# Strassen's algorithm for half the columns of an MLP's second projection, with the scale of u applied earlier

## The chip, the cores and the metric

The kernel runs on one core of one Trainium2 chip. A core has TensorE (PE in the profile, with its weight loads as PEld), VectorE (DVE), ScalarE (ACT), GpSimd (POOL), and SyncE (SP), whose queue issues nearly all the DMAs here. The metric is the device time of one execution in microseconds; lower is better.

## The reference

Two layers of an encoder on x of 256 tokens by 2048. Each layer adds to x the output projection of three kinds of attention heads, then a squared-ReLU MLP; a final RMSNorm ends it. What the change touches is the MLP:

```python
x = x + jnp.einsum('bse,ed->bsd', mix, w_o[l])
h = rmsnorm(x, norm_mlp[l])
u = jax.nn.relu(jnp.einsum('bsd,df->bsf', h, w_up[l]))
x = x + jnp.einsum('bsf,fd->bsd', u * u, w_down[l])
```

w_up is 2048 x 8192 and w_down 8192 x 2048 per layer, all in float32.

## The kernel before

**Precision.** Every float32 operand is split into a high part (a cast to fp32r) and a low part (the rest). A product of two is three matmuls: high by high, low by high, high by low. Weights are split on the chip: `split` (L829 to L839) casts 128x1024 values on ScalarE (L836, `whi`) and subtracts on VectorE (L837, `wlo`).

**Steps.** The whole kernel is a list of steps, one for each 512 KB of weights: 128 partitions by 1024 values. The main loop (from L868) goes through them in order. For step i it loads raw weights (`wraw`, six buffers) up to step i + 6, splits up to step i + 1 into pairs of `whi` and `wlo` (four pairs), and then issues the step's matmuls. Between the steps, `tick` issues pieces of other work from a queue. The framework orders each engine's instructions by its own priorities from this order of issue, so the orders printed below are those of the built programs.

**The MLP.** There are 256 tokens, two blocks t of 128. The 8192 inner columns go in eight groups g of 1024. An *up step* takes two row blocks of 128 and 512 inner columns of w_up, which gives u transposed, in four banks: eight matmuls of 512 columns (high and low of h side by side) and eight of 256 (L644, L648). After eight up steps the result is added up, squared with relu (L659), and split into u's high and low parts in `uT`, one tile for 256 inner columns, so four tiles for a group (q in the new code counts them through the layer). A *down step* takes 256 inner rows (one tile of `uT`, index k) by 512 output columns (index j) of w_down. With the three products, two row blocks and two token blocks it is twelve matmuls of 512 columns, all through `mode_b` (the matmul is L465). After four steps, the two banks are added to x on VectorE (L684), scaled by r2, one over the mean square of x: since relu is squared, the norm's scale can come after.

The order is the up steps of group 0, then for each g the 16 up steps of group g + 1 and the 16 down steps of group g. One may also read it as 16 down steps of a group followed by the 16 up steps of the group after the next. The normed h comes in eight tiles `hT2`, two for each of the four 512-column pieces of x (`hprep`, TensorE transposes at L210, ScalarE L218, VectorE L221).

**PSUM.** Six single banks (tag `bank`) serve as `mm` and `tr` tiles, and two more as one tile `S` for attention scores, or in the MLP for half of the up steps.

Of the kernel before, what the change touches and what calls it, by code (L numbers as in the profile page):

```python
# [23 lines left out]
P = 128  # L24
D = 2048
# [18 lines left out]
def tile_trunk(ctx: ExitStack, tc: tile.TileContext, x_in, w_in, w_o, w_up, w_down,  # L44
               gains, rowp, t5, rpb, gfin, cst, onehot, out):
    nc = tc.nc
    LOOK_LOAD, LOOK_SPLIT, BUDGET = 7, 2, 2.2
    N_WARM = 6
    D_X, D_S, D_SS, D_T, D_PV, D_QK, D_RQ, D_RK, D_SQ = 6.0, 6.0, 7.0, 18.0, 6.0, 6.0, 24.0, 16.0, 6.0
# [17 lines left out]
    def mid(dt, *shape):  # L67
        return dp.tile([P, *shape], dt, tag="mid", bufs=6, name=nm("mid"))

# [22 lines left out]
    ones = cp.tile([P, 64], F32, name="ones")  # L92
    nc.vector.memset(ones, 1.0)
# [349 lines left out]
    def mix_rs(l, grp, acc, done):  # L443
        ps = tr_bank()
        for t in range(NT):
            nc.tensor.matmul(ps[:, t * 64:(t + 1) * 64], acc[:, t * P:(t + 1) * P], ones, start=True, stop=True)
# [9 lines left out]
    class Step:  # L456
        def __init__(self, src, kk, n, pre, mm):
            self.src, self.kk, self.n, self.pre, self.mm = src, kk, n, pre, mm

    def mode_b(banks, h_tile, wh, wl, sub, first, last, n=512, blocks=(0, 1)):  # L460

        def one(t, i, part):
            kk = sub[i]
            a = h_tile[i][:, int(part == "lh"), kk, t * P:(t + 1) * P]
            return nc.tensor.matmul(banks[t][:, 0:n], a, (wl if part == "hl" else wh)[:, i, :],  # L465
                                    start=first and i == 0 and part == "hh",
                                    stop=last and i == len(sub) - 1 and part == stop).ins
        if hook[0]:
            stop = "hl"
            for part in ("hh", "lh", "hl"):  # L470
                with pinned():
                    ins = [one(t, i, part) for t in blocks for i in range(len(sub))]
                last_pe[0] = ins[-1]
                if part == "hh":
                    hook[0]()
            return
        stop = "lh"
        for t in blocks:
            for i in range(len(sub)):
                for part in ("hh", "hl", "lh"):  # L480
                    one(t, i, part)
# [3 lines left out]
    def layer_steps(l):  # L485
# [6 lines left out]
        def mlp_rs():  # L492
            st["r2"] = small(2)
            nc.vector.reciprocal(st["r2"], mean_eps(st["ss2"], 4, 1.0 / D))
# [130 lines left out]
        uT = {}  # L625

        def up_steps(g):
            for c in range(2):
                fc = 2 * g + c
                box = {}  # L630
                for k in range(8):
                    def pre(k=k):
                        need((("mlp", l), k))

                    def mm(wh, wl, k=k, c=c, fc=fc, box=box):
                        if k == 0:
                            box["b"] = [mm_bank() for _ in range(2 if c else 4)]
                            if c:
                                sb = score_banks().rearrange("p (b i) n -> p b (i n)", i=2)
                                box["b"] += [sb[:, 0], sb[:, 1]]  # L640
                        ht = st["hT2"][k]
                        for kk in range(2):
                            for fs in range(4):
                                nc.tensor.matmul(box["b"][fs], wh[:, kk, fs * P:(fs + 1) * P], ht[:, kk, :],  # L644
                                                 start=k == 0 and kk == 0, stop=False, skip_group_check=True)
                        for kk in range(2):
                            for fs in range(4):
                                nc.tensor.matmul(box["b"][fs][:, 0:256], wl[:, kk, fs * P:(fs + 1) * P],  # L648
                                                 ht[:, kk, 0:256],
                                                 start=False, stop=k == 7 and kk == 1, skip_group_check=True)  # L650
                        if k == 7:
                            for b in range(2):

                                a = mid(F32, 512)
                                for i in range(2):
                                    o, ai = box["b"][2 * b + i], a[:, i * 256:(i + 1) * 256]
                                    nc.scalar.copy(ai, o[:, 256:512])
                                    nc.vector.tensor_add(ai, ai, o[:, 0:256])
                                nc.vector.scalar_tensor_tensor(a, a, 0.0, a, op0=ALU.max, op1=ALU.mult)  # L659
                                u = big(F32R, 2, 2, 256)  # L660
                                uf = u.rearrange("p s k c -> p s (k c)")
                                nc.scalar.copy(uf[:, 0, :], a)
                                nc.vector.tensor_sub(uf[:, 1, :], a, f(uf[:, 0, :]))  # L663
                                uT[2 * fc + b] = u
                    steps.append(Step(w_up[l, fc * 8 + k], 2, 512, pre, mm))

        def down_steps(g):
            for j in range(4):
                box = {}
                for k in range(4):  # L670
                    def mm(wh, wl, j=j, k=k, box=box):
# [5 lines left out]
                        mode_b(box["b"], hts, wh, wl, [0, 1], k == 0, k == 3, blocks=(0,) if final else (0, 1))  # L677
# [4 lines left out]
                        def evac(t):  # L682
                            xs = x[:, t, j * 512:(j + 1) * 512]
                            nc.vector.scalar_tensor_tensor(xs, box["b"][t], st["r2"][:, t:t + 1], xs,  # L684
                                                           op0=ALU.mult, op1=ALU.add)
                        if final:
# [3 lines left out]
                            for c in range(2):  # L690
                                cols = slice(c * 256, c * 256 + 256)
                                for i, (hts, vh, vl) in enumerate(box["w"]):
# [3 lines left out]
                                nc.vector.scalar_tensor_tensor(xs, tail[c][:, 0:256], st["r2"][:, 1:2], xs,  # L696
                                                               op0=ALU.mult, op1=ALU.add)
# [7 lines left out]
                    steps.append(Step(w_down[l, (g * 4 + j) * 4 + k], 2, 512, None, mm))  # L705

        up_steps(0)
        for g in range(8):
            if g < 7:
                up_steps(g + 1)  # L710
            down_steps(g)
# [47 lines left out]
    def bias_a(kv):  # L759
        tb = sp.tile([P, 4, 384], F32, tag="bias", bufs=2, name=nm("biasA"))  # L760
        nc.sync.dma_start(tb, bass.AP(tensor=avec.tensor, offset=avec.offset + kv * 4 * 512,
                                        ap=[[1, P], [512, 4], [1, 384]]))
        return tb

    def g_unit(l, st, kind, kv, qb, qT, kh, kl, V, bias=None, rq=None):
# [5 lines left out]
        u.bias = lambda b: bias[:, 2 * b:2 * b + 2, qb * P:qb * P + 256][:, :, ::-1]  # L771
# [12 lines left out]
    def b_unit(l, st, h0, qT, kh, kl):  # L784
# [6 lines left out]
        tb = sp.tile([P, 2, 6 * 127], F32, tag="bias", bufs=2, name=nm("biasB"))  # L791
        for rr in range(2):
            off = ((l * 8 + h0) * 15 + rr + 4) * 127
            nc.sync.dma_start(tb[64 * rr:64 * rr + 64, :, 0:699], bass.AP(
                tensor=rpb.tensor, offset=rpb.offset + off, ap=[[1, 64], [15 * 127, 2], [1, 699]]))
        tc_ = big(F32, 2, 6, 64)
        for h in range(2):
            nc.gpsimd.tensor_add(tc_[:, h], tb[:, h].rearrange("p (a b) -> p a b", b=127)[:, :, 0:64],
                                 mask_b.rearrange("p (o d) -> p o d", o=1).to_broadcast([P, 6, 64]))
# [20 lines left out]
    raw_t, hi_t, lo_t = {}, {}, {}  # L820

    def load(i, halves=False):
        s = steps[i]
        w = wp.tile([P, s.kk, s.n], F32, tag="wraw", bufs=6, name=nm("wraw"))
# [5 lines left out]
    def split(i):  # L830
        s = steps[i]
        w = raw_t.pop(i)
        h = wp.tile([P, s.kk, s.n], F32R, tag="whi", bufs=4, name=nm("whi"))
        lo = wp.tile([P, s.kk, s.n], F32R, tag="wlo", bufs=4, name=nm("wlo"))
# [7 lines left out]
    nl = ns = 0  # L842
# [8 lines left out]
    for i in range(1, 8):  # L851
        load_x(i * 256, (i + 1) * 256)
        if i < 6:
            load(i)
    nl = 6
# [8 lines left out]
    for i, s in enumerate(steps):  # L864
# [17 lines left out]
        while ns < min(len(steps), i + LOOK_SPLIT):  # L882
            split(ns)
            ns += 1
        s.mm(hi_t.pop(i), lo_t.pop(i))
        hook[0] = None
        if i == 2:
# [61 lines left out]

def _pack_inputs(inp):  # L950
# [11 lines left out]
    o["w_up"] = np.stack([np.concatenate([_pack(a["w_up"][l][:, j * 512:(j + 1) * 512], 2) for j in range(16)])  # L962
                          for l in range(L)])
    o["w_down"] = np.stack([np.concatenate([
        _pack(a["w_down"][l][g * 1024:(g + 1) * 1024, j * 512:(j + 1) * 512], 2)
        for g in range(8) for j in range(4)]) for l in range(L)])
# [41 lines left out]
```

## Time and profile before

| | us |
|---|---|
| three runs, median (lowest to highest) | 2056.87 (2056.75 to 2056.89) |
| the profiled execution, its own time | 2057.3 |
| the profiled execution, its span | 2055.5 |
| ScalarE busy (share of the span) | 1049.3 (51%) |
| GpSimd busy (share of the span) | 255.7 (12%) |
| HBM bytes read | 377.34 MB |

The span is from the first to the last instruction; the execution's own time is 1.8 us longer. The page's busy rows give for each engine its time at work. Matmuls are pipelined, and their ends are modelled, so a single 128x512 matmul is shown as 0.39 us long though the next starts 0.23 us after it: how fast TensorE runs is read from the chain in order of time, not from the length of a matmul. The chain follows the work that ended last back to what released it.

In time, layer 0 has its projections and attention up to about 321 us, its MLP to about 1037 us; layer 1 follows.

### The profile page before, as it was taken

How to read it: one execution, taken by the hardware profiler on the slowest of the kernel's cores; microseconds unless marked ns; L12 is line 12 of the kernel's file. 1: busy time of each engine (PE TensorE's matmuls, PEld its weight loads, DVE VectorE, ACT ScalarE, POOL GpSimd, SP SyncE). 2: the span in 40 equal slices, each digit the busy share in tenths (PEclk: the TensorE clock that was granted, in tenths of full speed). 3: DMA queues.
4: the chain of work that ended last, by engine and by line, in shares of the span. 5: the costliest groups of instructions: out<-in, count | busy, mean ns of one | idle time of the engine just before them, and what ended most of it. 6: DMA issues, size and time to landing. Idle time of an engine off the chain costs nothing.

```text
span 2055.5 us, 27430 instructions
## 1 busy us (share of the span) xinstructions
PE 2040.7 (99%) x10424; PEld 1737.5 (85%) x10424; DVE 1337.7 (65%) x1629; ACT 1049.3 (51%) x1544; POOL 255.7 (12%) x294
## 2 busy tenths in 40 slices
PE   9999999999999999999999999999999999999998
PEld 8888888888888888888888888888888888888887
DVE  6777976565565655656668789766565556556565
ACT  6667755444344443444557677554344444434444
POOL 0483420000000000000006744100000000000001
PEclk9999999999999999999999999999999999999999
DMA  8655565666666666666656463566656566665663
GB/s 292 193 166 143 169 188 180 189 191 188 195 186 194 191 187 195 188 193 193 185 180 186 144 181 124 182 185 187 195 185 195 187 194 192 186 195 189 193 211 123
DMA packets 108497, 381.26 MB, mean 185 GB/s; under 512 B 11939, under 2 KB 16291, under 8 KB 108364
## 3 DMA queue, kind: packets, MB, share of 16 engines
q1 hardware_dynamic: 107932, 378.41, 59.8%
q8 instruction: 82, 1.34, 0.3%
q10 hardware_dynamic: 432, 1.10, 0.1%
q14 instruction: 51, 0.42, 0.1%
HBM read 377.34 MB, written 2.11 MB: 185 GB/s over the span
## 4 chain that ended last, share of the span: by engine, by line
PE 94%; DVE 3%; ACT 1%; issue 1%; DVEq 0%; POOLq 0%; POOL 0%; ACTq 0%
PE mm L465 55%; PE mm L644 17%; PE mm L648 9%; PE S L644 6%; PE S L648 3%; PE tr L383 1%; PE tr L402 1%; PE tr L210 1%; DVE wlo L837 1%; ACT big L363 1%; PE S L342 1%; PE S L341 1%; DVE big L278 1%; DVE big L385 0%; PE tr L395 0%
## 5 line engine op out<-in xcount | busy, mean ns | idle before, releaser
L837 DVE TENSOR_TENSOR wlo<-wraw,whi 128x1024 fp32r<-128x1024 f32 (+1 forms) x697 | 863.1, 1241 | 643.6 <-ACT whi L836 639.2
L836 ACT CAST whi<-wraw 128x1024 fp32r<-128x1024 f32 (+1 forms) x697 | 730.0, 1050 | 892.6 <-PE mm L465 455.4
L465 PE MATMUL mm<-whi,big 128*128 128x512 f32 (+1 forms) x3600 | 1109.3, 386 | 0.0
L465 PEld LDWEIGHTS mm<-whi,big 128*128 128x128 f32 x3600 | 670.8, 188 | 133.5 <-ACT whi L836 1.8
L465 PE MATMUL mm<-wlo,big 128*128 128x512 f32 (+1 forms) x1800 | 689.6, 385 | 1.0 <-DVE wlo L837 1.0
L644 PE MATMUL mm<-big,whi 128*128 128x512 f32 x1536 | 417.0, 393 | 0.0
L465 PEld LDWEIGHTS mm<-wlo,big 128*128 128x128 f32 x1800 | 338.6, 188 | 66.3 <-DVE wlo L837 2.4
L644 PEld LDWEIGHTS mm<-big,whi 128*128 128x128 f32 x1536 | 272.9, 189 | 44.4
L648 PE MATMUL mm<-big,wlo 128*128 128x256 f32 x1536 | 245.0, 282 | 0.0
L648 PEld LDWEIGHTS mm<-big,wlo 128*128 128x128 f32 x1536 | 227.7, 190 | 20.0
L644 PE MATMUL S<-big,whi 128*128 128x512 f32 x512 | 158.6, 390 | 0.0
L374 POOL TENSOR_SCALAR big<-big,sm 128x256 f32<-128x256 f32 x128 | 89.4, 716 | 247.1 <-DVE sm L372 197.4
L644 PEld LDWEIGHTS S<-big,whi 128*128 128x128 f32 x512 | 96.2, 188 | 22.0
L246 POOL TENSOR_TENSOR sm<-sm,mhalf 128x2 f32<-128x2 f32 (+2 forms) x12 | 12.0, 996 | 786.8 <-DVE sm L241 766.9
L648 PE MATMUL S<-big,wlo 128*128 128x256 f32 x512 | 103.2, 283 | 0.0
L732 POOL TENSOR_TENSOR x<-x,big 128x512 f32<-128x512 f32 x6 | 8.6, 1452 | 714.9 <-ACT mid L739 714.9
L684 DVE SCALAR_TENSOR_TENSOR x<-mm,sm,x 128x512 f32<-128x512 f32 x127 | 89.2, 744 | 3.1 <-PE mm L465 3.1
L648 PEld LDWEIGHTS S<-big,wlo 128*128 128x128 f32 x512 | 79.4, 191 | 0.0
L363 ACT ACTIVATE big<-S,sm,rq 128x256 f32<-128x256 f32 x64 | 35.3, 562 | 40.0 <-DVE sm L349 33.9
L659 DVE SCALAR_TENSOR_TENSOR mid<-mid 128x512 f32<-128x512 f32 x64 | 44.0, 688 | 0.5
L663 DVE TENSOR_TENSOR big<-mid,big 128x512 fp32r<-128x512 f32 x64 | 42.7, 686 | 0.0
L385 DVE TENSOR_TENSOR big<-tr,big 128x512 fp32r<-128x512 f32 x64 | 41.4, 682 | 0.5
(125 smaller groups left out, 1098.7 us busy)
## 6 DMA issues: line engine op xcount, KB each, us to landing
wraw<-in_w_up_dram SPq DMA_DIRECT2D x256, 512.0 KB, 3.5
wraw<-in_w_down_dram SPq DMA_DIRECT2D x256, 512.0 KB, 3.5
wraw<-in_w_in_dram SPq DMA_DIRECT2D x119, 512.0 KB, 3.8
wraw<-in_w_o_dram SPq DMA_DIRECT2D x64, 512.0 KB, 4.0
biasB<-in_rpb_dram SPq DMA_DIRECT2D x16, 349.5 KB, 6.4
biasA<-avec SPq DMA_DIRECT2D x4, 768.0 KB, 4.7
x<-in_x_dram SPq DMA_DIRECT2D x8, 256.0 KB, 7.4
big<-in_gfin_dram SPq DMA_DIRECT2D x2, 512.0 KB, 4.5
```

The lines of the kernel that those rows point to most:

```text
L210: tr = nc.tensor.transpose(psv[:, kk, t, :], x[:, t, c0:c0 + P], ident).ins
L363: nc.scalar.activation(p[:, s, :], src[s], AF.Exp, bias=negm[:, s:s + 1], scale=u.rq[:, s:s + 1] if u.kind == "C" else 1.0, accum_out=sums ...
L374: nc.gpsimd.tensor_scalar(p[:, s, :], p[:, s, :], rs[:, s:s + 1], 1.0, op0=ALU.mult, op1=ALU.mult)
L385: nc.vector.tensor_sub(u.pl[:, kb, :], ps, f(u.ph[:, kb, :]))
L465: return nc.tensor.matmul(banks[t][:, 0:n], a, (wl if part == "hl" else wh)[:, i, :], start=first and i == 0 and part == "hh", stop=last a ...
L644: nc.tensor.matmul(box["b"][fs], wh[:, kk, fs * P:(fs + 1) * P], ht[:, kk, :], start=k == 0 and kk == 0, stop=False, skip_group_check=True)
L648: nc.tensor.matmul(box["b"][fs][:, 0:256], wl[:, kk, fs * P:(fs + 1) * P], ht[:, kk, 0:256], start=False, stop=k == 7 and kk == 1, skip_gr ...
L659: nc.vector.scalar_tensor_tensor(a, a, 0.0, a, op0=ALU.max, op1=ALU.mult)
L663: nc.vector.tensor_sub(uf[:, 1, :], a, f(uf[:, 0, :]))
L684: nc.vector.scalar_tensor_tensor(xs, box["b"][t], st["r2"][:, t:t + 1], xs, op0=ALU.mult, op1=ALU.add)
L836: act = nc.scalar.copy(h[:, part], w[:, part]).ins
L837: last_lo[0] = nc.vector.tensor_sub(lo[:, part], w[:, part], f(h[:, part])).ins
```

## The change

**Half of w_down by Strassen's algorithm (Winograd's form).** For groups 0 to 6 and output columns j = 0 and 1, the product of u (two token blocks by inner rows) and w_down (inner rows by two column pieces) is taken as a product of 2 x 2 blocks. A11, A12, A21, A22 are u's blocks (token block by odd or even inner block), B11 to B22 those of w_down. Seven products of blocks take the place of eight: P1 = A11 B11, P2 = A12 B21, P3 = S4 B22, P4 = A22 T4, P5 = S1 T1, P6 = S2 T2, P7 = S3 T3. The S are sums of u's blocks (`sums_of`, made and split when u is), and the T sums of weight blocks: T1 = B11 + B12, T2 = B22 + T1, T3 = B12 + B22, T4 = B21 + T2, with the signs in the S and in how a product is added to x. They are made on VectorE (`prep`, L815 to L832). Each product goes over the group's four pairs of inner blocks in two halves h of six matmuls (L802). Products that share a sum stay in the same bank, and each product's bank is added to or subtracted from one piece of x as it stands (L782).

Columns j = 2 and 3, and the whole of group 7, stay as they were. In these groups `mode_b` now reads all high parts of the weights first and the low parts last (`lo_last`).

**Order.** A group's 14 halves are put one at a time between 24 other steps: 8 down steps (j = 2, 3) and the 16 up steps of the next group.

**u scaled ahead.** Since blocks of different tokens are added up, u must be scaled first. `rows` makes a tile `rrow` with one over the root mean square of each token along its free axis, by two matmuls with a matrix of ones (L521). The evacuation of u multiplies by it (L670), and ScalarE squares (L673). x's sums become plain additions (L739).

**Up steps** now take four row blocks by 256 columns instead of two by 512: the same sixteen matmuls into two banks, and an evacuation every four steps.

**Buffers.** `whi` and `wlo` get three pairs instead of four, `wraw` five buffers instead of six. A pair `spare` is the fourth pair in the projections and in group 7, and holds B11 in the other groups. Four tiles `side` hold B12, B22, B21, and the attention's biases, which had a pool of their own. In the MLP a step's weights are split two steps ahead of it.

The diff, cut:

```diff
-    LOOK_LOAD, LOOK_SPLIT, BUDGET = 7, 2, 2.2
+    LOOK_LOAD, LOOK_SPLIT, LOOK_PREP, BUDGET = 7, 2, 5, 2.2
...
+        if lo_last:
+            stop = "hl"
+            for part in ("hh", "lh", "hl"):
+                for t in blocks:
+                    for i in range(len(sub)):
+                        one(t, i, part)
+            return
...
+                    nc.vector.scalar_tensor_tensor(
+                        a, a, 0.0, rrow.rearrange("p (o c) -> p o c", o=1).to_broadcast([P, 2, 256]),
+                        op0=ALU.max, op1=ALU.mult)
+                    nc.scalar.activation(a, a, AF.Square, bias=zero1[:, 0:1])
...
+            nc.vector.tensor_sub(sm[:, 0:2, :], v[:, 0:4:3, :], v[:, 1:2, :].to_broadcast([P, 2, P]))
+            nc.vector.scalar_tensor_tensor(sm[:, 2, :], sm[:, 1, :], -1.0, a11, op0=ALU.mult, op1=ALU.subtract)
+            nc.vector.scalar_tensor_tensor(sm[:, 3, :], sm[:, 2, :], -1.0, a12, op0=ALU.mult, op1=ALU.subtract)
+            t = big(F32R, 2, 4, P)
+            nc.scalar.copy(t[:, 0], sm)
+            nc.vector.tensor_sub(t[:, 1], sm, f(t[:, 0]))
...
+            plan = [("P1", "A11", "a", True, (0, 0, 1)), ("P6", "S2", "a", False, (1, 0, 1)),
+                    ("P7", "S3", "d", True, (1, 1, -1)), ("P5", "S1", "a", False, (1, 1, -1)),
+                    ("P3", "S4", "a", False, (0, 1, -1)), ("P2", "A12", "b", True, (0, 0, 1)),
+                    ("P4", "A22", "d", False, (1, 0, 1))]
...
+                        for a, w in ((0, wh), (1, wh), (0, wl)):
+                            for i in range(2):
+                                nc.tensor.matmul(o, ops[i][a], w[:, i, :], skip_group_check=True,
...
+            order = [0, 0]
+            for p_ in range(7):
+                order += [1, 0, 1] + ([0, 0] + [0] * (p_ in (1, 3, 5)) if p_ < 6 else [])
...
-        w = wp.tile([P, s.kk, s.n], F32, tag="wraw", bufs=6, name=nm("wraw"))
+        w = wp.tile([P, s.kk, s.n], F32, tag="wraw", bufs=5, name=nm("wraw"))
...
-        h = wp.tile([P, s.kk, s.n], F32R, tag="whi", bufs=4, name=nm("whi"))
-        lo = wp.tile([P, s.kk, s.n], F32R, tag="wlo", bufs=4, name=nm("wlo"))
+            h = wp.tile([P, s.kk, s.n], F32R, tag="whi", bufs=3, name=nm("whi"))
+            lo = wp.tile([P, s.kk, s.n], F32R, tag="wlo", bufs=3, name=nm("wlo"))
...
-        while ns < min(len(steps), i + LOOK_SPLIT):
+        while ns < min(len(steps), i + LOOK_SPLIT + (not s.fourth)):
```

**How instructions move.** VectorE before, in the down steps of a middle group of layer 0: `wlo` is a split's subtract, `x<-mm` a result added to x.

```order
L837 TENSOR_TENSOR wlo_7044<-wraw_6945,whi_7043 128x1024
L684 SCALAR_TENSOR_TENSOR x<-mm_6951,sm_3379,x 128x512
L684 SCALAR_TENSOR_TENSOR x<-mm_6952,sm_3379,x 128x512
L837 TENSOR_TENSOR wlo_7062<-wraw_6965,whi_7061 128x1024
L837 TENSOR_TENSOR wlo_7080<-wraw_6983,whi_7079 128x1024
L837 TENSOR_TENSOR wlo_7100<-wraw_7001,whi_7099 128x1024
```

VectorE now, at the change from P1 to P6 in a middle group. `S_6126` is P1's bank, `mm_6086` and `mm_6087` those of j = 2, `big_6142` and `big_6176` the two halves of T2, `wlo_6195` the split of the second step of j = 3.

```order
L989 TENSOR_TENSOR wlo_6159<-wraw_6080,whi_6158 128x1024
L782 TENSOR_TENSOR x<-x,S_6126 128x512
L989 TENSOR_TENSOR wlo_6172<-big_6142,whi_6171 128x1024
L815 TENSOR_TENSOR spare_6028<-spare_6028,side_6133 128x1024
L739 TENSOR_TENSOR x<-x,mm_6086 128x512
L817 TENSOR_TENSOR big_6176<-side_6135,spare_6028 128x1024
L739 TENSOR_TENSOR x<-x,mm_6087 128x512
L989 TENSOR_TENSOR wlo_6195<-wraw_6120,whi_6194 128x1024
```

Where four splits in a row stood between two pairs of results, a product's result, a pair of results, and two sums of weights now stand between two splits.

TensorE now, at P7's first half (S3 by T3), between two up steps; `big_5661` and `big_5789` are the split sums of two tiles of u.

```order
L696 MATMUL mm_6296<-big_3209,wlo_6255 128x256
L802 MATMUL S_6126<-whi_6272,big_5661 128x512
L802 MATMUL S_6126<-whi_6272,big_5789 128x512
L802 MATMUL S_6126<-whi_6272,big_5661 128x512
L802 MATMUL S_6126<-whi_6272,big_5789 128x512
L802 MATMUL S_6126<-wlo_6273,big_5661 128x512
L802 MATMUL S_6126<-wlo_6273,big_5789 128x512
L691 MATMUL mm_6295<-big_3243,whi_6291 128x512
```

Before, sixteen up steps stood in a row and sixteen down steps of twelve matmuls; now a half of six stands between them, with a pair of split weights of its own.

VectorE now, a little later: `big_6142<-side_6508` (L832) makes P4's weights from B21 (`side_6508`), whose load is one of the latest issued.

```order
L989 TENSOR_TENSOR wlo_6273<-side_6100,whi_6272 128x1024
L821 TENSOR_TENSOR side_6133<-side_6133,side_6135 128x1024
L739 TENSOR_TENSOR x<-x,mm_6198 128x512
L739 TENSOR_TENSOR x<-x,mm_6199 128x512
L989 TENSOR_TENSOR wlo_6292<-wraw_6222,whi_6291 128x1024
L832 TENSOR_TENSOR big_6142<-side_6508,big_6142 128x1024
L989 TENSOR_TENSOR wlo_6316<-side_6133,whi_6315 128x1024
```

The sum of P4, the last product, stands ahead of the split of P7's second half, and `side_6508` takes the buffer of `side_6100`, which the first of these rows is the last to read.

More of the change, by code (lines that the diff above doesn't have):

```diff
@@ L456, in tile_trunk, with __init__, mode_b @@
     class Step:
-        def __init__(self, src, kk, n, pre, mm):
-            self.src, self.kk, self.n, self.pre, self.mm = src, kk, n, pre, mm
-    def mode_b(banks, h_tile, wh, wl, sub, first, last, n=512, blocks=(0, 1)):
+        def __init__(self, src, kk, n, pre, mm, fourth=True, loads=None, prep=None, raw=None, post=None):
+            self.src, self.kk, self.n, self.pre, self.mm, self.fourth = src, kk, n, pre, mm, fourth
+            self.loads, self.prep, self.raw, self.post = loads or [], prep, raw, post
+    def mode_b(banks, h_tile, wh, wl, sub, first, last, n=512, blocks=(0, 1), lo_last=False):
         def one(t, i, part):
@@ L492, in mlp_rs, with rows @@
         def mlp_rs():
-            st["r2"] = small(2)
-            nc.vector.reciprocal(st["r2"], mean_eps(st["ss2"], 4, 1.0 / D))
+            r = rsqrt(mean_eps(st["ss2"], 4, 1.0 / D), 2)
+            def rows():
+                dg = mid(F32, 2, P)
+                for t in range(NT):
+                    nc.vector.tensor_scalar(dg[:, t, :], ident, r[:, t:t + 1], None, op0=ALU.mult)
+                ps = tr_bank()
+                for t in range(NT):
+                    nc.tensor.matmul(ps[:, t * P:(t + 1) * P], full, dg[:, t, :], start=True, stop=True)
+                nc.vector.tensor_copy(rrow, ps[:, 0:256])
+                flags.add(("rrow", l))
+            add(rows, 0.45, delay=D_R, front=True)
         st["rs_mix"] = rs_mix
@@ L622, in layer_steps @@
                     steps.append(Step(src, 2, 512, pre, mm))
-        uT = {}
+        uT, sT = {}, {}
         def up_steps(g):
-            for c in range(2):
-                fc = 2 * g + c
+            out_, evacs = [], []
+            for q in range(4 * g, 4 * g + 4):
                 box = {}
[L631 to L665, printed above, removed]
@@ L669, in down_steps @@
+        def down_steps(g, js):
+            out_ = []
+            for j in js:
                 box = {}
@@ new lines, in layer_steps @@
+        steps.extend(up_steps(0))
+        for g in range(7):
+            ss = down_steps(g, (2, 3)) + up_steps(g + 1)
+            hs = strassen_steps(g)
+            order = [0, 0]
+            for p_ in range(7):
+                order += [1, 0, 1] + ([0, 0] + [0] * (p_ in (1, 3, 5)) if p_ < 6 else [])
+            assert order.count(0) == len(ss) and order.count(1) == len(hs), (order.count(0), order.count(1))
+            steps.extend(hs.pop(0) if o else ss.pop(0) for o in order)
+        steps.extend(down_steps(7, range(4)))
@@ L759, in bias_a @@
     def bias_a(kv):
[L760 to L763, printed above, removed]
+        pair = []
+        for h in range(2):
+            tb = side()[:, 0:768].rearrange("p (h k) -> p h k", h=2)
+            nc.sync.dma_start(tb, bass.AP(tensor=avec.tensor, offset=avec.offset + (kv * 4 + 2 * h) * 512,
+                                          ap=[[1, P], [512, 2], [1, 384]]))
+            pair.append(tb)
+        return pair
     def g_unit(l, st, kind, kv, qb, qT, kh, kl, V, bias=None, rq=None):
```

183 lines of the change are left out of this document (151 added, 32 removed).

## The prediction

> **What bounds the kernel now.** I read the page first, the chain of work that ended last, then the MLP by windows, then VectorE's instructions in order of time.
>
> ```profile
> span 2055.5 us, 27430 instructions
> PE 2040.7 (99%) x10424; PEld 1737.5 (85%) x10424; DVE 1337.7 (65%) x1629; ACT 1049.3 (51%) x1544; POOL 255.7 (12%) x294
> PEclk9999999999999999999999999999999999999999
> PE 94%; DVE 3%; ACT 1%; issue 1%; DVEq 0%; POOLq 0%; POOL 0%; ACTq 0%
> ```
>
> TensorE is busy for 2040.7 of 2055.5 us at full granted clock, and the chain is made of it. A busy PE could still be a slow PE, so its pace has to come from the chain in order of time:
>
> ```profile
> 676.37 43.55 PE mm L465 x192
> 764.59 43.55 PE mm L465 x192
> 676.37:764.59 88.22, 88.22 (x450) 75.37 (x449) 51.87 (x56) 38.16 (x45) 0.00 (x0) 1.00 0.62 191
> 719.92:764.59 44.67, 44.67 (x258) 39.33 (x257) 24.20 (x26) 19.97 (x23) 0.00 (x0) 1.00 0.63 190
> ```
> The windows' columns are the window, its length, then busy us of PE, PEld, VectorE, ScalarE, POOL, the clock, the DMA share and GB/s. One MLP group (16 down steps, then 16 up steps) lasts 88.22 us, and its 192 down matmuls run without a gap in 43.55 us: 0.2268 us each, 2.722 us for a step of 12. The 16 up steps take 44.67 us, 2.79 us each. In the group VectorE has 51.87 us of work, ScalarE 38.16. So a matmul taken out is worth 0.2268 us, as long as the other two engines still deliver.
>
> **What is removed.** In seven of a layer's eight groups, columns 0 to 1023 of w_down cost 2 x 4 steps x 12 = 96 matmuls; now seven products in two halves of 6, 84. That is 12 x 7 groups x 2 layers = 168 matmuls, or 168 x 0.2268 = **38.1 us**. A half takes 6 x 0.2268 = 1.36 us; the group becomes 44.67 + 8 x 2.722 + 14 x 1.361 = 85.50 us. Each half still accumulates six 128x512 matmuls into one bank, as L465 does now six times in a row, so the pace is the row's. The Trainium skill ("TensorE: Matmul & The Clock Gate", Back-to-back issue gap) gives N/2.4 + 2.5 ns for a warm matmul, 216 ns at 512 columns; by it the gain would be 36.3 us. The trace's pitch is longer, and I use that.
>
> **What is added on VectorE, per group.** These rows give durations, and how close one instruction can start behind another:
>
> ```profile
> L837 DVE TENSOR_TENSOR wlo<-wraw,whi 128x1024 fp32r<-128x1024 f32 x695 | 861.8, 1242 | 643.6 <-ACT whi L836 639.2
> L658 DVE TENSOR_TENSOR mid<-mid,mm 128x256 f32<-128x256 f32 x96 | 35.8, 415 | 0.0
> L659 DVE SCALAR_TENSOR_TENSOR mid<-mid 128x512 f32<-128x512 f32 x64 | 44.0, 688 | 0.5
> L663 DVE TENSOR_TENSOR big<-mid,big 128x512 fp32r<-128x512 f32 x64 | 42.7, 686 | 0.0
> L684 DVE SCALAR_TENSOR_TENSOR x<-mm,sm,x 128x512 f32<-128x512 f32 x127 | 89.2, 744 | 3.1 <-PE mm L465 3.1
> L286 DVE SCALAR_TENSOR_TENSOR mid<-mm,sm,mid 128x128 fp32r<-128x128 f32 x4 | 1.4, 351 | 0.7 <-ACT mid L284 0.7
> ...
> 676.54 1.23 DVE L837 TENSOR_TENSOR wlo<-wraw,whi 128x1024 fp32r<-128x1024 f32 x1 [1.57 <-ACT whi L836]
> 677.68 0.75 DVE L658 TENSOR_TENSOR mid<-mid,mm 128x256 f32<-128x256 f32 x2
> ...
> 681.47 1.29 DVE L663 TENSOR_TENSOR big<-mid,big 128x512 fp32r<-128x512 f32 x2
> 686.87 1.40 DVE L684 SCALAR_TENSOR_TENSOR x<-mm,sm,x 128x512 f32<-128x512 f32 x2
> ```
> The split's subtract lasts 1.23, but the next instruction starts 1.14 after it (677.68 - 676.54). In the same way a 512-wide result costs 1.40 - 0.74 = 0.66, an L663 or L659 0.60, an L658 0.34, a 128x128 about 0.26 (0.351 less the 0.09 of overlap). The new group has:
> - 38 splits (24 whole steps, 14 halves) instead of 32: 38 x 1.14 = 43.3
> - 8 sums of weight blocks (L815, L817, L821, L832). The trace shows no plain fp32 sum of this size; the nearest row is the split's subtract, the same shape with fp32r out: 8 x 1.14 = 9.1. Ends: half of it, and double (18).
> - 11 results into x (7 products, 4 whole) instead of 8: 11 x 0.66 = 7.3
> - 4 evacuations of u: 4 x (0.68 + 0.60 + 0.60) = 7.5, as before
> - 4 times the sums of u: one 256-wide pair sum 0.34, two 128x128, one 512 split 0.60: 4 x 1.46 = 5.8
>
> Sum 73.0 us of 85.50; by full durations 81.3. So VectorE gains over 20 us of work and stays below TensorE, on average. By full durations 4.2 us are spare, by starts, which I take, 12.5.
>
> The Trainium skill ("VectorE: DVE Perf Modes", The DRAIN you can't avoid) says that the next VectorE instruction does not start until the pipe is empty. By that rule the sum is 81.3, and the cover worked out below 0.5 us where I count 1.1; the trace disagrees by the 0.09 us of overlap above.
>
> **Whether an average is enough.** VectorE is in order, so a result that waits for TensorE holds up every split behind it; and the weight pairs fall from four to three.
>
> ```profile
> 706.36 1.05 ACT L836 CAST whi<-wraw 128x1024 fp32r<-128x1024 f32 x1 [1.67 <-PE mm L465]
> 707.45 1.23 DVE L837 TENSOR_TENSOR wlo<-wraw,whi 128x1024 fp32r<-128x1024 f32 x1 [1.50 <-ACT whi L836]
> ```
> The cast starts when a pair comes free and the subtract 1.09 us later. With three pairs that release comes from three steps back, so at worst 1.36 + 2.72 = 4.08 us remain for 1.05 + 1.14. But down steps of these groups now read the high part first and the low part in the last third (L486 on), as up steps do already: the pair's high half comes free about 0.9 us before a whole step ends, and the low half is needed only 1.81 us into it. I followed VectorE's new order through the group with these prices. The tightest place is the first pair of VectorE lists above. From the end of P1 (10.89 us into the group: three whole steps, two halves) VectorE has the result of P1, P6's split, two sums of weights, two results, another sum and then the split of the second j = 3 step: 3 x 0.66 + 4 x 1.14 = 6.54 us; the split sits behind about 1 us of backlog, so it ends near 18.4. TensorE wants that low part at five whole steps and three halves plus 1.81: 13.61 + 4.08 + 1.81 = 19.50. **About 1.1 us is left**; by full durations 0.5. I take no wait. If that cover fails, each us missing costs 14 us in all.
>
> The second place is the early L832, which waits for a load of B21:
>
> ```profile
> wraw<-in_w_down_dram SPq DMA_DIRECT2D x256, 512.0 KB, 3.5
> ```
> That load's buffer comes free only with P7's first split, near 25.8 us. It lands 3.5 later at 29.3, the sum ends at 30.4 and the split behind it at 31.6; TensorE wants its low part near 35.0. Spare 3.4. The bytes are unchanged (32 loads of 512 KB, DMA share 0.62), all through SP.
>
> ScalarE gets 6 casts, 4 squares and 4 small casts: 6 x 1.05 + 4 x 0.72 + 4 x 0.62 = 11.7 on 38.16, 50 of 85.5; bounds nothing.
>
> ```profile
> L199 ACT ACTIVATE mid<-x,zero 128x512 f32<-128x512 f32 x32 | 22.9, 721 | 0.6 <-DVE x L618 0.6
> L662 ACT CAST big<-mid 128x512 fp32r<-128x512 f32 x64 | 38.4, 620 | 1.7
> ```
>
> **Edits outside the groups.** An up step now reads four row blocks, so the last hT2 pieces are wanted at the fourth step instead of the seventh.
>
> ```profile
> 321.23 2.07 PE L644 MATMUL mm<-big,whi 128*128 128x512 f32 x8
> ...
> 325.42 1.59 ACT L218 ACTIVATE big<-tr,gn 128x256 fp32r<-128x256 f32 x4
> 326.71 1.65 DVE L221 SCALAR_TENSOR_TENSOR big<-tr,gn,big 128x256 fp32r<-128x256 f32 x4
> ...
> 307.93 0.87 PE tr L210 x8
> ...
> wraw<-in_w_o_dram SPq DMA_DIRECT2D x64, 512.0 KB, 4.0
> ```
> They are ready at 328.4; the fourth step would start at 321.2 + 3 x 2.79 + 0.87 = 330.5. Covered by 2.1 us, once per layer; without that cover up to 2 us a layer. The row of 1/rms costs TensorE four matmuls in all (L521): between 0.11 each (0.87/8, a 128-column fp32 transpose) and 0.23; I take 0.5 us together. Its VectorE and POOL parts lie beside the first up steps, and the first result is put off by a step. Five raw buffers instead of six shorten the load lead from 6 to 5 steps (16.3 to 13.6 us) against 4.0 to landing in the slowest weight row; weight loads keep their order up to the startup's fifth. The bias loads become 32 and 8 instead of 16 and 4, with the same bytes. I take 0 for these, with ends of -2 and +5 us, since the scheduler also rearranges the attention.
>
> **Sum.** The profiled execution took 2057.3 us (span 2055.5 and 1.8 around it), 0.4 above the median of 2056.87. 2057.3 - 38.1 + 0.5 = 2019.7; against the median **2019.3 us**.
>
> **The rivals.**
> 1. *VectorE is late at some places of a group.* For it: 0.5 to 1.1 us of cover, and eleven results that wait for TensorE. Against: two thirds of a step of cover added by the low-part-last order. At 1.2 us a group: 14 x 1.2 = 17, 2036 us; with 0.3 to 2.3 a group, 2024 to 2052.
> 2. *VectorE's queue becomes the period.* By full durations it has 81.3 us; if each of the 11 results blocks it for 0.8 us with nothing to do, a group takes 81.3 + 8.8 = 90.1 instead of 88.22, and the kernel 2057 + 14 x 1.9 = 2083 us. It decides from 88.2 - 81.3 = 6.9 us of such blocking a group, 0.63 a result. For: the order is fixed. Against: a backlogged VectorE finds its results ready and does not block. The sums of weights at double price would do the same.
> 3. *The halves don't run at the pitch*: six matmuls, then another stationary source and bank. 0.194 us lost per half eats all of it: 2057. Against it: the down and up steps alternate now without a gap at 676.37.
>
> **How the numbers follow.** Forecast (2016 to 2024): 0.72. Rival 1: 0.15. Rival 2: 0.09. Rival 3: 0.04. The range of 2014 to 2036 takes the forecast with its ends and half of rival 1. About 0.2%, 4 us, is what a measurement of this kernel can tell from no change. Faster 0.87, same 0.04, slower 0.09.
>
> **What would show it.** TensorE's busy time near 2003 us, 99% of the span; a group of 85.5 us; matmul count down by 164; VectorE near 73 to 78 us a group with idle time left. Rival 1 shows as TensorE or its weight load waiting for L989 or L988 at the same steps of every group, rival 2 as VectorE over 95% busy or idle behind L782, rival 3 as halves longer than 1.36 us.

## The result and the profile after

| | before | after |
|---|---|---|
| median of the runs, us | 2056.84 (4 runs, 2056.75 to 2056.89) | 2019.78 (4 runs, 2019.68 to 2019.96) |
| ratio, 95% interval | | 0.982 (0.9803 to 0.9837) |
| span of the profiled execution, us | 2055.5 | 2018.2 |

The change takes 37.1 us off the median and 37.3 us off the profiled span. The page of the changed kernel, its lines on the span, the engines and the chain's shares:

```profile
span 2018.2 us, 27873 instructions
PE 2003.0 (99%) x10264; PEld 1707.6 (85%) x10264; DVE 1644.0 (81%) x2095; ACT 1208.2 (60%) x1748; POOL 257.2 (13%) x296
PE 93%; DVE 3%; ACT 1%; POOL 1%; issue 1%; DMA 1%; SPq 0%; DVEq 0%; POOLq 0%
```

TensorE is busy for 37.7 us less and still for 99% of the span. VectorE has 306 us more work and the chain gives it the same 3%. One group by windows (length, then busy us of PE, PEld, VectorE, ScalarE and POOL, the clock, the DMA share and GB/s):

```profile
640.24:725.73 85.49, 85.49 (x437) 73.17 (x437) 73.66 (x90) 49.14 (x58) 0.00 (x0) 1.00 0.62 197
```

A group of the new kernel lasts 85.49 us where it lasted 88.22, and TensorE is busy for all of it. From the first half product of a group to that of the next it is 85.49 us all twelve times that two groups of a layer follow each other, so none of them shows a wait of its own. The chain in order of time (start, length, what) from the end of that group into the next:

```profile
709.41 5.44 PE mm L477 x24
714.85 1.36 PE S L802 x6
716.21 2.72 PE mm L477 x12
718.93 1.36 PE S L802 x6
720.29 5.44 PE mm L477 x24
725.73 1.36 PE S L802 x6
727.09 2.72 PE mm L477 x12
```

L802 are the half products, L477 the plain down steps. Each piece starts where the one ahead of it ends, and six matmuls of a half take 1.36 us. At the start of a layer, where the four new matmuls (L521) stand between the up steps, the same view shows:

```profile
327.86 1.84 PE mm L691 x8
329.70 0.95 PE mm L696 x8
330.65 0.44 PE tr L521 x4
331.09 1.85 PE mm L691 x8
```

No gap there either: the four cost 0.44 us in a layer. The code has two of them a layer, and each stands as two in the trace. VectorE's instructions in order of time, at the two places that the prediction called tight:

```profile
721.25 0.68 DVE L782 TENSOR_TENSOR x<-x,S 128x512 f32<-128x512 f32 x1
721.85 1.22 DVE L989 TENSOR_TENSOR wlo<-big,whi 128x1024 fp32r<-128x1024 f32 x1
...
726.45 1.22 DVE L989 TENSOR_TENSOR wlo<-wraw,whi 128x1024 fp32r<-128x1024 f32 x1
727.59 1.22 DVE L989 TENSOR_TENSOR wlo<-big,whi 128x1024 fp32r<-128x1024 f32 x1
...
739.96 1.23 DVE L832 TENSOR_TENSOR big<-side,big 128x1024 f32<-128x1024 f32 x1 [1.12 <-DMA side<-in_w_down_dram]
```

The subtract at 726.45 is the tight one. It ends at 727.67. The step that reads it starts at 727.09 in the chain and wants the low part after eight of its matmuls, 1.81 later, at 728.90: 1.2 us are left. In the chain a matmul starts where the one ahead of it ends; by the matmul's own row, which overlaps the one ahead, it is 1.07 us:

```profile
728.74 1.07 PE L477 MATMUL mm<-wlo,big 128*128 128x512 f32 x4
```

At 739.96 the sum L832 starts 1.12 us late because its load landed late; no matmul waits for it. The row of such loads on the page (count, KB each, median us from issue to landing):

```profile
side<-in_w_down_dram SPq DMA_DIRECT2D x84, 512.0 KB, 4.3
```

The new VectorE work by line (count, then busy us, mean ns of one, and idle time before it):

```profile
L832 DVE TENSOR_TENSOR big<-side,big 128x1024 f32<-128x1024 f32 x28 | 34.3, 1225 | 29.3 <-DMA side<-in_w_down_dram 29.3
L815 DVE TENSOR_TENSOR spare<-spare,side 128x1024 f32<-128x1024 f32 x28 | 34.1, 1218 | 0.0
L782 DVE TENSOR_TENSOR x<-x,S 128x512 f32<-128x512 f32 x84 | 57.2, 681 | 0.1
```

A sum of weights lasts as long as a subtract of a split, and a result into x (L782) 0.68 us.

### The profile page after: what moved, and what is told of

Its sections match the earlier page's. It is cut to its first block, busy times and chain, and to the rows that moved or that the text cites. A ratio compares the mean times of both kernels' runs of the same rounds, so it can differ in the third digit from the quotient of the medians.

```text
span 2018.2 us, 27873 instructions
## 1 busy us (share of the span) xinstructions
PE 2003.0 (99%) x10264; PEld 1707.6 (85%) x10264; DVE 1644.0 (81%) x2095; ACT 1208.2 (60%) x1748; POOL 257.2 (13%) x296
## 4 chain that ended last, share of the span: by engine, by line
PE 93%; DVE 3%; ACT 1%; POOL 1%; issue 1%; DMA 1%; SPq 0%; DVEq 0%; POOLq 0%
PE mm L477 40%; PE mm L691 23%; PE mm L696 12%; PE S L802 11%; PE mm L802 2%; PE tr L392 1%; PE tr L219 1%; POOL big L939 1%; DVE wlo L989 1%; PE tr L411 1%; ACT big L372 1%; DVE big L287 1%; PE S L351 1%; PE S L350 1%; DVE big L394 0%
## 5 line engine op out<-in xcount | busy, mean ns | idle before, releaser
L988 ACT CAST whi<-wraw 128x1024 fp32r<-128x1024 f32 (+1 forms) x531 | 556.9, 1051 | 421.9 <-PE mm L691 170.2
L989 DVE TENSOR_TENSOR wlo<-wraw,whi 128x1024 fp32r<-128x1024 f32 (+1 forms) x531 | 655.9, 1237 | 184.7 <-ACT whi L988 181.8
L477 PE MATMUL mm<-whi,big 128*128 128x512 f32 (+1 forms) x2252 | 643.8, 386 | 0.3 <-ACT whi L988 0.3
L477 PEld LDWEIGHTS mm<-whi,big 128*128 128x128 f32 x2252 | 419.0, 188 | 82.9 <-ACT whi L988 2.3
L691 PEld LDWEIGHTS mm<-big,whi 128*128 128x128 f32 x2048 | 377.4, 188 | 73.7
L477 PE MATMUL mm<-wlo,big 128*128 128x512 f32 (+1 forms) x1126 | 375.7, 385 | 1.0 <-DVE wlo L989 1.0
L477 PEld LDWEIGHTS mm<-wlo,big 128*128 128x128 f32 x1126 | 212.0, 188 | 41.8 <-DVE wlo L989 2.3
L802 PE MATMUL S<-whi,big 128*128 128x512 f32 x672 | 182.3, 393 | 0.0
L477 PE MATMUL mm<-spare,big 128*128 128x512 f32 (+1 forms) x678 | 158.5, 382 | 0.0
L477 PEld LDWEIGHTS mm<-spare,big 128*128 128x128 f32 x678 | 122.3, 188 | 23.1
L802 PEld LDWEIGHTS S<-whi,big 128*128 128x128 f32 x672 | 119.2, 189 | 18.6
L802 PE MATMUL S<-wlo,big 128*128 128x512 f32 x336 | 104.0, 391 | 0.0
```

What stands on the lines that cost most here:

```text
L802: nc.tensor.matmul(o, ops[i][a], w[:, i, :], skip_group_check=True, start=fresh and h == 0 and i == 0 and a == 0 and w is wh, stop=h == 1 ...
L988: act = nc.scalar.copy(h[:, part], w[:, part]).ins
L989: last_lo[0] = nc.vector.tensor_sub(lo[:, part], w[:, part], f(h[:, part])).ins
```

## The experiments

What had to be told apart: is the gain the removed matmuls alone; does the cover at the tight place hang on the order of low parts; how far is VectorE from being the limit, and is it its sum over a group or a place in the group that decides.

**1. Low parts in the old order.** The plain down steps again take the three products of each row and token block in turn, so that the weights are read high, low, high.

```diff
-                               lo_last=g < 7)
+                               lo_last=False)
```

> The whole steps of a Strassen group read high and low parts in turn again. Theory (the tight place after P1 has 1.2 us of cover, and that cover rests on reading the low parts last): the low part is wanted 1.81 - 0.23 = 1.58 us earlier there, so about 0.4 us is missing, and more because a pair comes free later in the step; 0.4 to 1.5 us a group, 6 to 21 us in all, 2025 to 2041 us. Rival (VectorE was never near the edge, the order of the parts does not matter): 2019.8, within 2 us.

Measured: 2021.75 us (2021.63 to 2022.2), ratio 0.983 (0.9815 to 0.9844). The 6 us or more of the theory did not come, and the rival's number holds, 2.0 us being at its edge. The rival's reason does not hold: the cover is gone, as the trace shows. The chain of this kernel in order of time, at the place that was tight:

```profile
725.88 1.36 PE S L802 x6
727.25 0.45 PE mm L477 x2
727.70 0.61 PE S L802 x2
728.31 2.41 PE mm L477 x10
730.71 0.91 PE S L802 x4
```

and VectorE's subtract for the plain step there:

```profile
726.87 1.22 DVE L989 TENSOR_TENSOR wlo<-wraw,whi 128x1024 fp32r<-128x1024 f32 x1
```

The scheduler, which sets the order when the kernel is built, answered the edit: a second matmul of a high part and two matmuls of the next half now stand ahead of the plain step's first low one. The low part is ready at 726.87 + 1.22 = 728.09, and the weight load that reads it had to wait for it:

```profile
728.14 0.19 PEld L477 LDWEIGHTS mm<-wlo,big 128*128 128x128 f32 x1 [0.28 <-DVE wlo L989]
```

So nothing is left of the 1.2 us, and it costs little all the same: this group (the window 714.84 to 800.63) lasts 85.79 us, the one before it (629.32 to 714.84) 85.52, where the changed kernel has 85.49. Without the move the low part would have been wanted behind the step's first matmul, at 727.25 + 0.23 = 727.48, and been 0.6 us late. In the first group of the first layer TensorE waits longer. The chain of this kernel there:

```profile
382.91 1.23 DVE big L817
...
384.23 1.06 ACT whi L988
...
385.34 1.19 PE S L802 x4
386.53 2.28 PE mm L477 x10
```

It runs through VectorE and ScalarE up to 385.34, where the changed kernel's runs through TensorE alone. From the layer's first L521 (330.15 here, 330.65 in the changed kernel) to the end of this stretch (394.71 and 394.64) the order costs 0.57 us. The second layer's first group (1373.93 to 1460.00) lasts 86.07 us, 0.58 more than in the changed kernel. The rest of the 2.0 us is spread, and was not followed.

**2 to 4. The subtract done twice in some halves.** The second one writes the same values again. 1.14 us of VectorE are added for each half: in P5 and P3, in the middle of the group and behind the tight place (4 halves, 4.6 us per group), in P1 and P6 (4.6 us too), three of whose four halves are split ahead of the tight place, and in all seven products (16.0 us). The three differ only in the names:

```diff
-                    stp = Step(None, 2, 512, None, mm, fourth=False, prep=prep, raw=get,
+                    stp = Step(None, 2, 512, None, mm, fourth=False, prep=prep, raw=get, twice=name in ("P5", "P3"),
...
-            last_lo[0] = nc.vector.tensor_sub(lo[:, part], w[:, part], f(h[:, part])).ins
+            for _ in range(1 + s.twice):
+                last_lo[0] = nc.vector.tensor_sub(lo[:, part], w[:, part], f(h[:, part])).ins
```

In P5 and P3:

> The split's subtract is done twice in the four halves of P5 and P3: 4 x 1.14 = 4.6 us more VectorE work a group, 78.2 instead of 73.7 of 85.5 us, at places where the ledger has more than a step of room. Theory (VectorE counts by its starts, and only places matter): no wait, 2019.8 within 1 us. Rival (VectorE counts by full durations, 81 us + 4.9 = 86 of 85.5, so the average binds): at least 0.7 us a group, 2030 us or more.

Measured: 2023.39 us (2022.55 to 2023.46), ratio 0.9836 (0.9822 to 0.9851). 64 us of VectorE work (14 x 4.6) cost 3.6 us. The theory said 1 at most and missed by about 2.6; the rival by full durations is out. The trace shows where part of it goes: weight loads of the halves wait for VectorE's low part 8 times, 3.9 us in all, and never in the changed kernel. In five of the fourteen groups it is P5's first half that takes 1.47 to 1.63 us in the chain in place of 1.39: its second subtract stands behind the sum L832 (two lines lower here), which waits for its load.

In P1 and P6:

> The same 4.6 us of VectorE work a group, but in the four halves of P1 and P6, around the place that has 1.2 us of cover. Theory (the place decides): three of the four doubled subtracts stand ahead of the split that is wanted there, 3.4 us against 1.2 of cover, less what the scheduler moves: 0.5 to 2.2 us a group, 2027 to 2051 us. Rival (only VectorE's total matters): the same as with P5 and P3.

Measured: 2041.72 us (2041.3 to 2042.8), ratio 0.9927 (0.9911 to 0.9944). The same work, most of it ahead of the tight place, costs 21.9 us, six times as much. The waits of this kernel (us in total, times, longest):

```profile
PEld mm L479 <- DVE wlo L992: 16.4, 18, 1.1
PE mm L479 <- DVE wlo L992: 9.1, 14, 0.7
```

A group of it by windows:

```profile
640.00:727.11 87.11, 86.29 (x438) 72.88 (x437) 77.91 (x94) 49.02 (x58) 0.00 (x0) 1.00 0.62 194
```

L479 and L992 are the plain down step and the subtract, two lines lower than in the changed kernel. TensorE's matmuls of the plain steps wait for a low part 14 times, as many as there are groups, and the group grows by 1.62 us: 14 x 1.62 = 22.7, near the 21.9 (the first group of the first layer, 372.73 to 459.32, grows by only 1.10). VectorE is busy for only 77.91 of 87.11 us. It isn't its sum that costs here, but its place.

In all seven:

> The subtract twice in all 14 halves: 16 us more a group, 73.7 + 16.0 = 89.6 us of VectorE work by starts against 85.5 of TensorE. Theory (VectorE's queue becomes the period, the slower rival of the prediction made real): a group of 89.6 us or more, 14 x 4.1 = 57 us or more, at least 2077 us, slower than the kernel before; VectorE over 95% busy in the groups. By full durations (98.7 us a group) 2204 us. If VectorE had much more room than counted: below 2040 us.

Measured: 2060.8 us (2060.27 to 2061.31), ratio 1.0019 (1.001 to 1.0028), so slower than before the change. A group by windows:

```profile
640.00:728.70 88.70, 86.41 (x438) 72.79 (x437) 88.02 (x104) 48.66 (x58) 0.00 (x0) 1.00 0.61 190
```

Here VectorE is the period: 88.02 of 88.70 us. 104 instructions, 14 more than without the doubles; 88.02 - 14 x 1.14 = 72.1 us is what a group of the changed kernel needs on VectorE when nothing makes it wait. The theory's direction was right and its group 0.9 us too long, because it had counted 73.7 us for that. Full durations, the rival, are far off.

**5. P4's matmuls left out.**

```diff
-                        for a, w in ((0, wh), (1, wh), (0, wl)):
+                        for a, w in () if name == "P4" else ((0, wh), (1, wh), (0, wl)):
```

> P4's 12 matmuls of every group are left out (its halves are still loaded, summed and split; the columns that use P4 come out without it): 14 steps of half size, 14 x 2.722/2 x 2 = 38.1 us of TensorE over the kernel, 2.72 us of each group (85.49 to 82.77). Theory A (TensorE alone bounds, VectorE's 71.9 us per group have room everywhere): 2019.8 - 38.1 = 1981.7 us, 1979 to 1985. Theory B (the 1.2 us of cover behind P1 and what lies around P4 are about all there is; with 2.7 us less TensorE in that stretch the low parts come late): 1 to 2.7 us of each of 7 groups come back, 1989 to 2010 us, with TensorE waits on VectorE's low parts in every group.

Measured: 1982.3 us (1982.11 to 1982.34), ratio 0.9635 (0.9621 to 0.965). That is 75.0 us under the kernel before in the same series (2057.29), and so 37.9 us more than the change's own 37.1. A group by windows:

```profile
643.20:725.97 82.77, 82.77 (x425) 70.86 (x425) 73.22 (x90) 48.74 (x59) 0.00 (x0) 1.00 0.64 203
```

Theory A holds: the group falls by the whole 2.72 us and TensorE is busy for all of it, with VectorE's work unchanged. The 1.2 us at the tight place is not the margin of the whole group: another 2.7 us of TensorE work per group went at P4 without any wait.

**6. Everything but the products.** All columns plain, no sums of u; u scaled ahead, the new up steps, the buffers and the order of low parts stay.

```diff
-                if q < 28:
+                if False:
...
-            ss = down_steps(g, (2, 3)) + up_steps(g + 1)
-            hs = strassen_steps(g)
+            steps.extend(down_steps(g, range(4)) + up_steps(g + 1))
+            continue
...
-    if g < 7:
+    if g < 0:
```

> All columns of w_down plain in all groups, no sums of u; the rest of the change stays (u scaled by 1/rms ahead, the new order of up steps, buffers, the order of low parts). Theory: the 168 removed matmuls are the whole gain and the other edits cost the 0.9 us that the transposes show in the profile: 2056.9 + 0.9 = 2057.8 us, 2056.5 to 2059. Rival: the other edits give or take several us of their own (part of the 37 us is from them): under 2055 or over 2061 us.

Measured: 2058.23 us (2057.85 to 2058.53) beside 2057.29 for the kernel before in the same series, ratio 1.0004 (0.9995 to 1.0014). The other edits together are worth nothing that can be told from no change, 0.9 us by the medians, and the L521 rows account for 2 x 0.44 of it. A group by windows is as before:

```profile
676.00:764.20 88.20, 88.20 (x449) 75.37 (x448) 52.17 (x57) 40.83 (x49) 0.00 (x0) 1.00 0.61 191
```

From this kernel to the changed one only the products, their sums and the order of steps that goes with them differ. Each taken against the kernel before in its own series, that is 37.06 + 0.94 = 38.0 us; 38.1 were forecast for the 168 matmuls.

**7. The sums of weights on GpSimd.** Since VectorE is the next limit, its 8 sums per group were moved, and prepared two steps earlier.

```diff
-    LOOK_LOAD, LOOK_SPLIT, LOOK_PREP, BUDGET = 7, 2, 5, 2.2
+    LOOK_LOAD, LOOK_SPLIT, LOOK_PREP, BUDGET = 7, 2, 7, 2.2
...
-                            nc.vector.tensor_add(raw["B11", h], raw["B11", h], raw["B12", h])
+                            nc.gpsimd.tensor_add(raw["B11", h], raw["B11", h], raw["B12", h])
...
-                            nc.vector.tensor_add(t2[h], raw["B22", h], raw["B11", h])
+                            nc.gpsimd.tensor_add(t2[h], raw["B22", h], raw["B11", h])
...
-                            nc.vector.tensor_add(raw["B12", h], raw["B12", h], raw["B22", h])
+                            nc.gpsimd.tensor_add(raw["B12", h], raw["B12", h], raw["B22", h])
...
-                            nc.vector.tensor_add(t2[h], raw["B21", h], t2[h])
+                            nc.gpsimd.tensor_add(t2[h], raw["B21", h], t2[h])
```

> The 8 sums of w_down's quarters of a group run on GpSimd in place of VectorE. VectorE falls by 8 x 1.14 = 9.1 us per group (71.9 to 62.8 by starts). Theory: TensorE bounds, VectorE's time is idle time anyway: 2019.8 us, 2018 to 2022. Rival: GpSimd's sums (nearest row 1.45 to 1.6 us for half the size, so 2.9 to 3.2 us each, about 25 us per group) come late for the splits or hold up VectorE's own operations: 1 us or more per group, 2027 us or more.

Measured: 2119.03 us (2118.71 to 2119.91), ratio 1.0301 (1.0286 to 1.0316). The theory fell and the rival won, by far: 61.7 us over the kernel before, so 99 over the changed one. A group by windows:

```profile
647.66:740.30 92.64, 88.02 (x438) 73.46 (x437) 80.21 (x82) 48.91 (x59) 23.19 (x8) 0.98 0.58 182
```

VectorE (DVE) and GpSimd (POOL) of this kernel in order of time:

```profile
740.30 3.35 POOL L815 TENSOR_TENSOR spare<-spare,side 128x1024 f32<-128x1024 f32 x1 [50.37 <-DVE wlo L989]
741.43 2.76 DVE L676 TENSOR_TENSOR big<-mid,big 128x512 fp32r<-128x512 f32 x1
743.73 2.72 POOL L821 TENSOR_TENSOR side<-side,side 128x1024 f32<-128x1024 f32 x1
744.12 2.61 DVE L712 TENSOR_TENSOR mid<-mid 128x256 f32<-128x256 f32 x1
746.41 2.54 POOL L817 TENSOR_TENSOR big<-side,spare 128x1024 f32<-128x1024 f32 x1
746.76 2.33 DVE L713 SCALAR_TENSOR_TENSOR mid<-mid,mid 128x128 f32<-128x128 f32 x1
749.13 0.29 DVE L714 SCALAR_TENSOR_TENSOR mid<-mid,mid 128x128 f32<-128x128 f32 x1
...
751.08 6.74 DVE L989 TENSOR_TENSOR wlo<-wraw,whi 128x1024 fp32r<-128x1024 f32 x2
...
756.70 3.39 POOL L821 TENSOR_TENSOR side<-side,side 128x1024 f32<-128x1024 f32 x1
757.75 0.67 DVE L782 TENSOR_TENSOR x<-x,S 128x512 f32<-128x512 f32 x1
```

VectorE had 9.1 us of work taken away (82 instructions instead of 90), and is busy for 80.21 us instead of 73.66. While a GpSimd sum runs, a VectorE instruction that reads two SBUF operands ends only some tenths of a us behind it, in the rows here 0.14 to 0.54. L712 lasts 2.61 (0.42 in the changed kernel), L713 2.33 (0.29), L676 2.76 (0.69); L714 starts 0.2 us behind the end of GpSimd's sum (746.41 + 2.54), with none running, and takes its usual 0.29. L782 at 757.75 reads one operand from PSUM (S), and takes its usual 0.67 under a running GpSimd sum. The first three, none of which uses a result of GpSimd, lose 2.07 + 2.19 + 2.04 = 6.3 us. The chain of this kernel in order of time goes right through them:

```profile
739.07 1.06 ACT whi L988
...
741.43 2.76 DVE big L676
744.20 2.54 DVE mid L712
...
746.76 2.35 DVE mid L713
...
749.34 1.23 DVE wlo L989
...
751.35 6.37 PE mm L477 x20
```

TensorE waits 2.97 us for the split that is queued behind them. So at this place it was the holding up and not a sum that came too late; the group is 7.15 us longer, and 14 x 7.15 = 100 us is the loss. It goes on behind this place: two splits take 6.74 us from 751.08, and TensorE waits another 1.23 us at 761.22. How the loss divides among the places was not taken apart. TensorE also ran slower for a moment, in the 20 matmuls of the last row: from 751.50 to 754.90 the granted clock was 0.50, and a stretch like it lies behind the 0.98 of the window above. That is not the cause of the loss: a group without such a stretch, 464.54 to 557.21 at a clock of 1.00, lasts 92.67 us. The Trainium skill ("SBUF — State Buffer", SBUF: two separate sides) has this rule: VectorE and GpSimd share a port pair of SBUF, taken by one for a whole instruction, and a VectorE instruction with two SBUF inputs waits for a GpSimd one that reads SBUF. The trace agrees, with 2.33 us for an instruction of 0.29, and with the one that has a PSUM operand as the exception.

## Why the prediction was right

Forecast 2019.3 us, measured 2019.78.

- *The removed matmuls.* 38.1 us forecast. Measured: 14 groups shorter by 88.22 - 85.49 = 2.73, so 38.2 us in all, and 38.0 between experiment 6 and the changed kernel. The row's pitch of 0.2268 us was the right price. By the 216 ns of the Trainium skill ("TensorE: Matmul & The Clock Gate", Back-to-back issue gap) it would have been 36.3, and the runs do not agree with that. The section gives the 216 ns for a single isolated matmul, which the prediction leaves out, and about 131 ns for a stream of them; by an estimate from that it would be 22.0 us, which is further off. Rival 3 (halves off the pitch) is out by the chain: 1.36 us each, and 1.39 behind an up step.
- *The row of 1/rms.* 0.5 us forecast in all; measured 2 x 0.44 = 0.88. The step was right, the size off by 0.4 us: a matmul of L521 costs 0.11, the lower of the two ends that stood there, but there are four in each layer and not in all, which is also why the matmul count fell by 160 (10424 to 10264) and not by 164. This is most of the distance to the forecast.
- *The rest outside the groups.* Taken at 0 with ends of -2 and +5; experiment 6 measures 0.9 with the L521 matmuls in it, so 0. What the scheduler makes of the attention could not be worked out beforehand, so that it came to nothing is in part luck.
- *VectorE's sum.* Forecast 73.0 us by starts and 81.3 by durations, and by starts taken. Experiment 4, which makes VectorE the period, shows 72.1. The 0.9 lie mostly in the results: 11 at 0.66 forecast, and 721.85 - 721.25 = 0.60 measured, and they are plain additions now that no longer carry a scale. The weight sums, priced by the nearest row at 1.14, hold: 724.12 - 722.98 = 1.14 for L815 between its start and the next instruction's, and 1.22 long. The Trainium skill ("VectorE: DVE Perf Modes", The DRAIN you can't avoid) says that the next instruction does not start until the pipe is empty. As the prediction used it, that would make it the 81.3 us; the 14 doubles would then have cost 14 x 1.22 on top of that, and experiment 4's group would be 98.4 us. It is 88.70. The same section adds, and the prediction leaves out, that a next instruction that is not held starts earlier.
- *The tight place.* Forecast 1.1 us of cover, measured 1.2 by the chain and 1.07 by the matmul's own row. The prediction's sentence names three sums of weights on the way there; its list of VectorE's order has two, as its term 4 x 1.14 counts. That the place is the right one is shown by experiments 2 and 3: the same 4.6 us cost 21.9 us in all (three quarters of them ahead of it) and 3.6 behind it. The reason given beside it, "two thirds of a step of cover added by the low-part-last order", holds for the cover and not for the time: without that order the cover is gone, but the kernel loses 2.0 us and not a wait of 0.4 us or more in each group, since the scheduler put other matmuls in the way. The hand calculation held the order of the matmuls fixed, and it wasn't.
- *"If that cover fails, each us missing costs 14 us in all."* Experiment 3: 1.62 us per group, 21.9 in all, 13.5 per us.
- *The load of B21.* The sum was forecast to start at 29.3 us into the group and starts at 739.96 - 709.41 = 30.55, and by the medians 0.8 of the 1.25 us are the loads' 4.3 us, for which 3.5 had been taken from the plain weights' row. The spare of 3.4 us took it.
- *Rival 2* (VectorE's queue as the period) was priced to decide from 6.9 us of extra work or blocking a group. Experiment 4 got there with 16 us, since starts count and not durations (88.22 - 72.1 = 16.1). It is a real mechanism, and 2060.8 us is its time.

## What to carry to other kernels

Removing TensorE work pays at the pitch of the trace as long as the engine that feeds it keeps up at every place, so price the feeder by the distance between starts and follow its queue to the tightest place. Work put on VectorE mostly ahead of that place cost six times what the same work cost behind it. Read a dependence on an edit only with the scheduler's answer to it: here it replaced a cover by reordering.

No version faster than the changed kernel that computes the same came out of the runs. Strassen for the other half of the columns would add to VectorE 6 splits, 8 sums and 3 results, 14 x 1.14 + 3 x 0.60 = 17.8 us on 72.1, so 89.9 us per group, over the 85.49 of now; that is worked out and was not run.

## What the runs showed of the hardware

- GpSimd's 128x1024 fp32 sums of two SBUF operands took 2.8 to 3.1 us on average, and held up VectorE instructions with two SBUF operands: three of them by 2.0 to 2.2 us each, down to one of 0.29 us (to 2.33). It turned 9.1 us less VectorE work into 6.6 us more busy time per group.
- Back-to-back VectorE instructions overlap by 0.08 us (1.22 long, next start after 1.14); over a group of 90 to 104 instructions that is 7 to 8 us, the difference between a VectorE that has room and one that has hardly any.
